# Hybrid encoder trunk: one modulation sum of the first layer moved from two half tiles ahead of a PSUM pool's closing to behind the half tile that follows the closing

## The chip, the cores and the metric

The kernel runs on one core of one Trainium2 chip. The metric is the device time of one launch in microseconds (us), as the median of the runs shown. One further launch was taken with the hardware profiler; the rows quoted below come from it, and times in rows count from the start of its span.

## The reference

Two layers on 1024 tokens of width 1024, one batch. In each layer a condition vector gives six modulation vectors (shift, scale and gate, for attention and for the feed-forward part); the input is normalised and modulated; ONE projection makes queries, keys and values of three head groups (A neighbourhood, B sliding window, C dense); each group's attention, a norm, an output projection and a gated sum follow, and then a gated SwiGLU part.

```python
cond = jax.nn.silu(c)
for l in range(DEPTH):
    mod = cond @ w_mod[l] + b_mod[l]
    sh_a, sc_a, gt_a, sh_f, sc_f, gt_f = [m[:, None, :] for m in split_cols(mod, (D,) * 6)]
    h = rms_norm(x, g_attn[l]) * (1 + sc_a) + sh_a
    proj = h @ w_in[l]
...
    x = x + gt_a * (y @ w_o[l])
    h = rms_norm(x, g_ffn[l]) * (1 + sc_f) + sh_f
...
    x = x + gt_f * ((jax.nn.silu(gate) * up) @ w_down[l])
return rms_norm(x, g_final)
```

## The kernel before, in words

Every matrix product is made of three TensorE (PE) passes, since each operand is split in a high and a low part (`mm3`: high by high, low by high, high by low). A product's PSUM tile fills one of the eight banks.

**The stage around the change** is the last part of the projection in the first layer (`l == 0`), in which the columns of groups A and B are projected. Column tiles `oc` 2 to 7, each in two halves of 512 tokens, make twelve half tiles, numbered `i = 2 * (oc - NE) + half`, 0 to 11 (two of them were computed earlier, in the start of the kernel). For each half tile:

- `ab_proj` makes 24 matmuls 128x512 into a PSUM tile `ps_ab` (8 pieces of the sum, 3 passes each);
- `ab_split` has ScalarE (ACT) cast the high part out of that PSUM tile into `qko`, and VectorE (DVE) subtract to get the low part. That DVE instruction, `qko<-ps_ab,qko`, is the tile's last reader and sets its bank free;
- `store` puts `qko` into DRAM (`qkd`), with DMAs that ACT's queue issues one half tile later, behind DVE's instruction;
- at the first half of each column tile, `split_tile` prepares the next tile's weights: ACT casts `whi`, DVE subtracts `wlo`.

**The modulation** of later stages is computed between these on DVE, which has time left. `mod_one` loads one block of 128 rows of `w_mod` (`wmt`, 512 KB, three buffers) and adds it, times the condition, to `acc` (128x1024). After the eighth block it splits `acc` into `acch` and `accl`. `mod_sum` then adds up the 128 partitions: four PE matmuls by a matrix of ones into two PSUM tiles `ps_mod`, and on DVE, twice, a product by the identity into `own` and a reduction into `sums`, and at the end a small addition into `mods`. A table sets for each half tile how many `mod_one` follow, and a tuple sets at which half tiles a `mod_sum` stands.

**The order is written by hand.** In this stage the five engines are pinned: what stands first in the code stands first in the engine's queue, and each engine works through its queue in order. An instruction that waits holds up all that stands behind it on that engine.

**Two PSUM pools.** Half tiles up to 7 take their tiles from a pool `psl` of eight banks. At `oc == 6`, first half (`i == 8`), this pool is closed, and two others open in its banks: `psS` with two tiles of two banks for the scores `sC`, and a new `psl` with four banks. A tile of a new pool waits for the last reader of what stood in its bank.

```python
1201         def mod_sum():
...
1204             l_, g, hi, lo = sums_due.pop(0)
...
1207             for o in (0, H):
1208                 ps = psl.tile([P, 4, P], F32, name="ps_mod", tag="mm")
...
1325                 if oc == 6 and half == 0:
1326                     close(ps_cm)
1327                     psS_cm, psS = open_pool("psS", bufs=2, space=PSUM)
1328                     ps_cm, psl = open_pool("ps2", bufs=4, space=PSUM)
...
1331                 ps = None if early else ab_proj(w, half)
...
1339                 if i in ((2, 6, 10) if l else (3, 6, 10)):
1340                     mod_sum()
```

With `oc == 7` (`i` 10 and 11) the first scores of group C stand in front of the half tile (`early_scores`): eight matmuls into two `sC` tiles, two maxima on DVE (`vecs<-sC`), two exponentials on ACT (`pr`, then `wst`), a reciprocal on DVE, and a division on GpSimd (POOL). After half tile 11 the four-bank pool closes too, and `opened` begins with attention of group C: transposes `T` (three banks), scores, and products `pv` (one bank).

Of the kernel before, what the change touches and what calls it, by code (L numbers as in the profile page):

```python
# [85 lines left out]
def trunk(ctx: ExitStack, tc, A, C, out):  # L86
# [9 lines left out]
    def open_pool(name, bufs=1, side="left", space=None):  # L96
        kw = dict(name=name, bufs=bufs, side=side, reuse_waits="tile")
        if space is not None:
            kw["space"] = space
            if space == PSUM:  # L100
                kw.pop("side")
        cm = tc.tile_pool(**kw)
        p = cm.__enter__()
        return cm, p

    def close(cm):
        cm.__exit__(None, None, None)
# [45 lines left out]
    def split_tile(st, a=1, hl=None, eng=None, scale=None):  # L153
        pl, tag, bufs = hl or (wp, "whl", 8)
        hi = pl.tile([P, 1024], F32R, name="whi", tag=tag, bufs=bufs)
        lo = pl.tile([P, 1024], F32R, name="wlo", tag=tag, bufs=bufs)
        if scale is None:
            act.copy(hi, st)
            (eng or pool).tensor_tensor(out=lo, in0=st, in1=f32(hi), op=ALU.subtract)
        else:  # L160
            act.activation(hi, st, AF.Copy, scale=scale)
            eng.scalar_tensor_tensor(
                out=lo, in0=st, scalar=scale, in1=f32(hi), op0=ALU.mult, op1=ALU.subtract
            )
        return parts(hi, a), parts(lo, a)
# [565 lines left out]
    def w_ab(l, oc):  # L731
        st = stage()
        c0 = oc * P if oc < 4 else 768 + (oc - 4) * P
        sp.dma_start(
            parts(st, KC), A["w_in"][l, :, c0 : c0 + P].rearrange("(k p) n -> p k n", p=P)
        )
        return st
# [167 lines left out]
    for l in range(2):  # L905
# [23 lines left out]
        def ab_proj(w, half):  # L929
            c = slice(half * H, (half + 1) * H)  # L930
            ps = psl.tile([P, 512], F32, name="ps_ab", tag="mm")
            for k in range(KC):
                mm3(ps, w[0][:, k], w[1][:, k], hh[:, k, c], hl[:, k, c], k == 0, k == 7)
            return ps

        def ab_split(oc, half, ps, pl):

            c = slice(half * H, (half + 1) * H)
            o = pl.tile([P, 2, H], F32R, name="qko", tag="qko", bufs=2)
            hi, lo = o[:, 0, :], o[:, 1, :]  # L940
            if oc < 4:
                hi, lo = (t.rearrange("p (j r i) -> p r j i", j=8, r=8) for t in (hi, lo))
                ps = ps.rearrange("p (r j i) -> p r j i", r=8, j=8)
                act.copy(hi, ps)
                sub(lo, ps, f32(hi))
            else:
                sc = -0.125 if oc < 7 else 1.0
                act.activation(hi, ps, AF.Copy, scale=sc)
                dve.scalar_tensor_tensor(
                    out=lo, in0=ps, scalar=sc, in1=f32(hi), op0=ALU.mult, op1=ALU.subtract  # L950
                )

            def store(eng=sp):
                for j in range(2):
                    to, v = qkd[oc, j], f32(o[j * 64 : j * 64 + 64])
                    if oc < 4:
                        to = to.rearrange("z p (j h n) -> h p z j n", h=2, n=64)[half]
                        v = v.rearrange("p z (j n) -> p z j n", n=64)
                        for z in range(2):
                            eng.dma_start(to[:, z], v[:, z])  # L960
                    else:
                        eng.dma_start(to[:, :, c].rearrange("z p t -> p z t"), v)

            return store
# [210 lines left out]
        def z_step():  # L1175
            if z_steps:
                what, h = z_steps.pop(0)
                what(h)
# [5 lines left out]
        def mod_one():  # L1184
            l_, g = todo[0]
            k = going["step"]
            if k == 0:
                going["acc"] = cp.tile([P, 1024], F32, name="acc", tag="acc")
            acc = going["acc"]
            mod_step(l_, g, k, acc, wm)  # L1190
            going["step"] = (k + 1) % KC
            if k == KC - 1:
                todo.pop(0)
                hi, lo = (
                    wp.tile([P, 1024], F32R, name=f"acc{p}", tag="whl", bufs=8) for p in "hl"
                )
                dve.tensor_copy(hi, acc)
                dve.tensor_tensor(out=lo, in0=acc, in1=f32(hi), op=ALU.subtract)
                sums_due.append((l_, g, hi, lo))

        def mod_sum():


            l_, g, hi, lo = sums_due.pop(0)
            sums = cp.tile([P, 8], F32, name="sums", tag="sums")
            own = wp.tile([P, 1024], F32, name="own", tag="whl", bufs=8)
            for o in (0, H):
                ps = psl.tile([P, 4, P], F32, name="ps_mod", tag="mm")
                row = ps.rearrange("p a b -> p (a b)")
                pe.matmul(row, onesr, hi[:, o : o + H], start=True, stop=False)  # L1210
                pe.matmul(row, onesr, lo[:, o : o + H], start=False, stop=True)
                d = own[:, o : o + H].rearrange("p (a b) -> p a b", a=4)
                dve.tensor_tensor(out=d, in0=ps, in1=bc(ident[:, None, :], [P, 4, P]), op=ALU.mult)
                n = o // P
                dve.tensor_reduce(out=sums[:, n : n + 4], in_=d, axis=AX.X, op=ALU.add)
            mod_finish(l_, g, sums)
# [86 lines left out]
        def early_scores():  # L1303

            p = len(first_pairs)
            if p == 0:
                prs = [
                    wp.tile([P, 1024], F32, name="pr", tag="whl", bufs=8),
                    cp.tile([P, 1024], F32, name="pr", tag="acc"),
                ]  # L1310
            else:
                prs = [stage(), stage()]
            rs = vecs[0][:, 8 * p : 8 * p + 8]
            for c in range(2):
                c_scores(0, 2 * p + c, c, prs[c], rs)
            first_pairs.append(prs)
            return lambda: divide(prs, rs)

        for oc in range(NE, 8):
            w = wab  # L1320
            for half in range(2):
                if half == 0 and oc < 7:
                    sc = -0.125 if oc < 3 else None
                    wab = split_tile(wst.pop(0), KC, eng=dve, scale=sc)
                if oc == 6 and half == 0:
                    close(ps_cm)
                    psS_cm, psS = open_pool("psS", bufs=2, space=PSUM)
                    ps_cm, psl = open_pool("ps2", bufs=4, space=PSUM)
                scored = early_scores() if oc == 7 else None
                early = l == 0 and half == 0 and oc in EARLY_AB  # L1330
                ps = None if early else ab_proj(w, half)
                if store:
                    store(sp if oc == 7 and half else act)
                if scored:
                    scored()
                if half == 0 and oc < 6:
                    wst.append(w_ab(l, oc + 2))
                i = 2 * (oc - NE) + half
                if i in ((2, 6, 10) if l else (3, 6, 10)):
                    mod_sum()  # L1340
                z_step()
                for _ in range(
                    (1, 1, 1, 1, 1, 1, 1, 1, 2, 2, 0, 0)[i]
                    if l else (0, 1, 0, 1, 2, 2, 2, 2, 2, 0, 0, 0)[i]
                ):
                    mod_one()
                store = None if early else ab_split(oc, half, ps, ab)
# [419 lines left out]
        for n in range(-AHEAD - 1, N + 3):  # L1767
# [84 lines left out]
            for end, (chunks, width) in norms.items():  # L1852
                if begins[end] <= m <= end and (m - begins[end]) % 8 == 7 and (n <= NC or m >= NC):
                    i = (m - begins[end]) // 8
# [569 lines left out]
        for u in range(NU):  # L2424
            i, t = divmod(u, NB)
# [164 lines left out]
```

## Time and profile before

| | |
|---|---|
| median of 3 runs | 2373.5 us |
| lowest and highest of them | 2372.1 and 2374.26 us |
| the profiled execution, whole | 2373.83 us |
| its span, first to last instruction | 2372.1 us |
| PE busy, its share of the span | 2327.3 us, 98% |
| DVE busy | 1755.5 us, 74% |
| ACT busy | 1184.2 us, 50% |
| POOL busy | 775.7 us, 33% |
| mean granted TensorE clock | 0.997 |

A timeline row gives start, duration, engine, operation, output<-inputs with shapes, the number of instructions merged, and in brackets how long the engine had stood idle before it and what ended that. PE rows of a single 128x512 matmul have a duration of 0.39 us but start 0.23 us apart, since matmuls overlap; the distance of starts is what counts. In rows all code has line L49, a helper that issues every instruction; groups are told apart by tile names. 1.73 us of the profiled execution (2373.83 less 2372.1) lie outside its span.

### The profile page before, as it was taken

Reading aid. Unit: us, or ns where it says so; the run is one execution under the profiler, and the core shown is the slowest. Engines: PE = TensorE matmul, PEld = TensorE weight load, DVE = VectorE, ACT = ScalarE, POOL = GpSimd, SP = SyncE. Lnnn points to the kernel's source line nnn. Section 1 sums busy time; section 2 is a strip of 40 time slices with the busy share of each in tenths; the row PEclk is TensorE's granted clock in tenths of the full one; section 3 lists DMA queues with packets and bytes.
Section 4 is the critical chain, followed back from the end, with each engine's and each line's share of the span. In section 5 each row is a group of like instructions: output and inputs, shape, how many; then the busy total and the mean of one; then the engine's idle time right before and its main releaser. Section 6 shows DMA issues by size and latency. Waiting matters only on the chain. (4 is left out here: it accounts for less than half of the span.)

```text
span 2372.1 us, 33468 instructions
## 1 busy us (share of the span) xinstructions
PE 2327.3 (98%) x11804; PEld 1960.9 (83%) x11804; DVE 1755.5 (74%) x2753; ACT 1184.2 (50%) x2261; POOL 775.7 (33%) x747
## 2 busy tenths in 40 slices
PE   9999999999999999999999999999999999999998
PEld 7887888888788888788888889988878888888886
DVE  6877998868857687596767689897796674537765
ACT  4422888844543333344533158896454334334443
POOL 1530356710344444200145124574005444430001
PEclk9999999999999999999999999999999999999999
DMA  8666507163345444686434861332634443239743
GB/s 279 182 204 199 156 5 210 39 212 107 111 155 164 152 142 151 201 248 186 153 102 128 252 187 28 91 104 89 221 98 130 154 153 103 98 105 294 213 120 112
DMA packets 307417, 358.02 MB, mean 151 GB/s; under 512 B 51996, under 2 KB 223868, under 8 KB 307248
## 3 DMA queue, kind: packets, MB, share of 16 engines
q1 hardware_dynamic: 290752, 346.26, 47.0%
q10 hardware_dynamic: 16128, 9.44, 1.5%
q8 instruction: 93, 1.52, 0.3%
q14 instruction: 76, 0.62, 0.1%
q0 software_dynamic: 368, 0.17, 0.0%
HBM read 270.84 MB, written 88.63 MB: 152 GB/s over the span
## 5 line engine op out<-in xcount | busy, mean ns | idle before, releaser
L49 PE MATMUL ps_d<-wpt 128*128 128x512 f32 x1848 | 423.7, 390 | 1.0 <-ACT wpt L49 0.7
L49 PEld LDWEIGHTS ps_d<-wpt 128*128 128x128 f32 x1848 | 345.7, 188 | 74.3 <-issue 3.0
L49 POOL TENSOR_SCALAR pr<-pr,rs 128x1024 f32<-128x1024 f32 (+2 forms) x248 | 190.5, 783 | 186.6 <-DVE rs L49 169.3
L49 POOL TENSOR_TENSOR sg<-sg,u 128x512 f32<-128x512 f32 x82 | 118.3, 1444 | 348.4 <-ACT sg L49 221.6
L49 PE MATMUL pv<-pt,vs 128*128 128x256 f32 x1088 | 173.9, 296 | 14.1 <-DVE y L49 12.9
L49 DVE TENSOR_TENSOR pt<-T,pt 128x512 fp32r<-128x512 f32 x272 | 177.3, 679 | 7.0 <-ACT pt L49 5.9
L49 ACT CAST wpt<-w 128x512 fp32r<-128x512 f32 x154 | 95.6, 621 | 167.8 <-PE ps_d L49 151.6
L49 DVE SCALAR_TENSOR_TENSOR acc<-wmt,condT,acc 128x512 f32<-128x512 f32 (+1 forms) x98 | 116.1, 1191 | 78.5 <-DMA wmt<-in_w_mod_dram 77.6
L49 ACT CAST pt<-T 128x512 fp32r<-128x512 f32 x272 | 151.5, 585 | 42.5 <-PE T L49 41.1
L49 ACT COPY u<-ps_w 128x512 f32<-128x512 f32 x128 | 75.1, 587 | 191.7 <-PE ps_w L49 189.5
L49 POOL TENSOR_TENSOR wpt<-ws,wpt 128x512 fp32r<-128x512 f32 x80 | 110.9, 1387 | 179.8 <-ACT wpt L49 139.3
L49 DVE TENSOR_TENSOR wpt<-w,wpt 128x512 fp32r<-128x512 f32 x154 | 108.7, 706 | 79.8 <-ACT wpt L49 79.7
L49 PEld LDWEIGHTS pv<-pt,vs 128*128 128x128 f32 x1088 | 141.0, 189 | 26.7 <-DVE y L49 24.6
L49 PE MATMUL T<-identr,pr 128*128 128x128 f32 x1176 | 160.0, 273 | 0.9 <-ACT edge L49 0.5
L49 PEld LDWEIGHTS T<-identr,pr 128*128 128x128 f32 x1176 | 137.8, 140 | 15.7 <-ACT edge L49 1.1
L49 ACT CAST wpt<-ws 128x512 fp32r<-128x512 f32 x176 | 107.7, 622 | 52.0 <-issue 23.0
L49 ACT CAST wpt<-graw 128x512 fp32r<-128x512 f32 x154 | 95.0, 617 | 59.2 <-DMA graw<-gpd 51.8
L49 DVE TENSOR_TENSOR wpt<-graw,wpt 128x512 fp32r<-128x512 f32 x154 | 109.8, 713 | 18.1 <-ACT wpt L49 18.1
L49 DVE TENSOR_TENSOR wpt<-ws,wpt 128x512 fp32r<-128x512 f32 x96 | 84.4, 887 | 47.7 <-ACT wpt L49 47.4
L49 DVE TENSOR_TENSOR ws<-wr 128x512 f32<-128x512 f32 x88 | 80.9, 919 | 50.4 <-POOL wpt L49 46.6
L49 DVE TENSOR_REDUCE rs<-sC 128x1 f32<-128x1024 f32 x88 | 107.4, 1220 | 12.8 <-PE sC L49 11.5
L49 PE MATMUL ps_w<-h22h,wpt 128*128 128x512 f32 x352 | 108.9, 391 | 2.4 <-ACT u L49 1.4
(306 smaller groups left out, 5932.1 us busy)
## 6 DMA issues: line engine op xcount, KB each, us to landing
wr<-in_w_gu_dram SPq DMA_DIRECT2D x92, 512.0 KB, 4.3
gpd<-sg SPq DMA_DIRECT2D x154, 256.0 KB, 4.4
graw<-gpd SPq DMA_DIRECT2D x76, 512.0 KB, 3.9
w<-in_w_down_dram SPq DMA_DIRECT2D x110, 256.0 KB, 5.2
wmt<-in_w_mod_dram SPq DMA_DIRECT2D x48, 512.0 KB, 5.5
qk<-qkd SPq DMA_DIRECT2D x44, 512.0 KB, 7.2
wst<-in_w_o_dram SPq DMA_DIRECT2D x32, 512.0 KB, 4.2
wmt<-in_w_mod_dram SPq DMA_DIRECT2D x64, 256.0 KB, 4.0
```

Source lines behind the costliest of these rows:

```text
L49: ins = op(*args, **kwargs)
```

## The change

In the first layer the second of three modulation sums stands at half tile 8 instead of 6. The table of `mod_one` is as it was, and so are the second layer and the queues of ACT, POOL and SP (their instructions keep their order).

```diff
                 i = 2 * (oc - NE) + half
-                if i in ((2, 6, 10) if l else (3, 6, 10)):
+                if i in ((2, 6, 10) if l else (3, 8, 10)):
                     mod_sum()
```

On PE, from half tile 6 (`ps_ab_1816`) on; the rows are the first of each tile, with the engines that they wait for (24 matmuls of each `ps_ab` are cut to one or two). First before:

```order
L49 MATMUL ps_ab_1816<-hh_111,whi_1727 128x512 [waits PE_49,Activation_49]
...
L49 MATMUL ps_mod_1847<-acch_1768,onesr_73 128x512 [waits DVE_49,PE_49]
L49 MATMUL ps_mod_1847<-accl_1769,onesr_73 128x512 [waits DVE_49]
L49 MATMUL ps_mod_1852<-acch_1768,onesr_73 128x512 [waits PE_49]
L49 MATMUL ps_mod_1852<-accl_1769,onesr_73 128x512
L49 MATMUL ps_ab_1867<-hh_111,whi_1727 128x512 [waits PE_49]
...
L49 MATMUL ps_ab_1914<-hh_111,whi_1812 128x512 [waits DVE_49]
```

Then with the change:

```order
L49 MATMUL ps_ab_1816<-hh_111,whi_1727 128x512 [waits PE_49,Activation_49]
...
L49 MATMUL ps_ab_1854<-hh_111,whi_1727 128x512 [waits PE_49]
...
L49 MATMUL ps_ab_1901<-hh_111,whi_1812 128x512 [waits PE_49,Activation_49]
L49 MATMUL ps_ab_1901<-hh_111,wlo_1813 128x512 [waits DVE_49]
...
L49 MATMUL ps_mod_1930<-acch_1768,onesr_73 128x512
L49 MATMUL ps_mod_1930<-accl_1769,onesr_73 128x512
L49 MATMUL ps_mod_1935<-acch_1768,onesr_73 128x512
L49 MATMUL ps_mod_1935<-accl_1769,onesr_73 128x512
```

The four matmuls of the sum moved past half tiles 7 (`ps_ab_1867`, now `ps_ab_1854`) and 8 (`ps_ab_1914`, now `ps_ab_1901`), and the waits in front of half tile 8 are others. In the built program before, half tile 7 lies in bank 4, and half tile 8, the first tile of the new four-bank pool, lies in bank 4 too: its wait on DVE is for `qko_1900<-ps_ab_1867`, the last reader of half tile 7. With the change half tile 7 lies in bank 1, and half tile 8 in bank 4, which held a `ps_mod` tile of the first sum; its waits are for PE's own matmuls of that sum, for ACT's `whi_1812` and for DVE's `wlo_1813`, the halves of its weights. The sum's two tiles lie in banks 7 and 6 of the new pool, and half tile 9 in bank 5.

On DVE, from the weights of half tile 8 (`wlo_1813`) on, first before (`qko_1864` and `qko_1900` read half tiles 6 and 7):

```order
L49 TENSOR_TENSOR wlo_1813<-wst_1760,whi_1812 128x1024
L49 TENSOR_TENSOR own_1846<-ps_mod_1847,identr_63 128x512
L49 TENSOR_REDUCE sums_1845<-own_1846 128x4
L49 TENSOR_TENSOR own_1846<-ps_mod_1852,identr_63 128x512
...
L49 SCALAR_TENSOR_TENSOR acc_1802<-wmt_1861,condT_79,acc_1802 128x1024
L49 SCALAR_TENSOR_TENSOR qko_1864<-ps_ab_1816,qko_1864 128x512
...
L49 SCALAR_TENSOR_TENSOR acc_1802<-wmt_1897,condT_79,acc_1802 128x1024
L49 SCALAR_TENSOR_TENSOR qko_1900<-ps_ab_1867,qko_1900 128x512
L49 TENSOR_TENSOR wlo_1904<-wst_1843,whi_1903 128x1024
L49 SCALAR_TENSOR_TENSOR acc_1802<-wmt_1941,condT_79,acc_1802 128x1024
```

Then with the change (`qko_1851` and `qko_1887` read half tiles 6 and 7, `qko_1951` half tile 8):

```order
L49 TENSOR_TENSOR wlo_1813<-wst_1760,whi_1812 128x1024
...
L49 SCALAR_TENSOR_TENSOR qko_1851<-ps_ab_1816,qko_1851 128x512
...
L49 SCALAR_TENSOR_TENSOR qko_1887<-ps_ab_1854,qko_1887 128x512
L49 TENSOR_TENSOR wlo_1891<-wst_1843,whi_1890 128x1024
L49 TENSOR_TENSOR own_1929<-ps_mod_1930,identr_63 128x512
L49 TENSOR_REDUCE sums_1928<-own_1929 128x4
...
L49 SCALAR_TENSOR_TENSOR acc_1802<-wmt_1941,condT_79,acc_1802 128x1024
L49 SCALAR_TENSOR_TENSOR acc_1802<-wmt_1944,condT_79,acc_1802 128x1024
L49 CAST acch_1947<-acc_1802 128x1024
L49 TENSOR_TENSOR accl_1948<-acc_1802,acch_1947 128x1024
L49 SCALAR_TENSOR_TENSOR qko_1951<-ps_ab_1901,qko_1951 128x512
```

The sum's five instructions moved past four `acc` steps, two `qko` and one `wlo`. In front of them now stands the wait for PE's sum behind half tile 8; behind them stand two `acc` steps, the two splits of `acc` and the last reader of half tile 8.

On PE again, where attention begins (`T` are the transposes of the first probabilities, `sC` scores); the last rows of the pieces show the waits, first before and then with the change:

```order
L49 MATMUL T_2133<-identr_63,pr_1984 128x128 [waits DVE_49,Pool_49]
L49 MATMUL T_2133<-identr_63,pr_1984 128x128 x3
L49 MATMUL T_2140<-identr_63,pr_1984 128x128 [waits DVE_49]
...
L49 MATMUL sC_2147<-qk_746 128x512 [waits Activation_49]
...
L49 MATMUL T_2152<-identr_63,pr_1985 128x128 [waits Pool_49]
...
L49 MATMUL T_2159<-identr_63,pr_1985 128x128 [waits DVE_49]
```

```order
L49 MATMUL T_2133<-identr_63,pr_1984 128x128 [waits DVE_49,Pool_49]
L49 MATMUL T_2133<-identr_63,pr_1984 128x128 x3
L49 MATMUL T_2140<-identr_63,pr_1984 128x128 x4
L49 MATMUL sC_2147<-qk_746 128x512 [waits Activation_49]
...
L49 MATMUL T_2152<-identr_63,pr_1985 128x128 [waits DVE_49,Pool_49]
...
L49 MATMUL T_2159<-identr_63,pr_1985 128x128 [waits DVE_49]
```

The order is the same, but `T_2152` waits for DVE as well. It lies in bank 5, which before held a tile of the third sum and with the change holds half tile 11; the wait is for that half tile's last reader. `T_2140` (bank 6) had to wait for the last reader of half tile 10, which now lies in bank 7.

## The prediction

> **What bounds the kernel now.** I read the page first, then the waits of PE, then the timeline of PE, DVE and ACT around the closing of the eight-bank pool.
>
> ```profile
> span 2372.1 us, 33468 instructions
> PE 2327.3 (98%) x11804; PEld 1960.9 (83%) x11804; DVE 1755.5 (74%) x2753; ACT 1184.2 (50%) x2261; POOL 775.7 (33%) x747
> ```
>
> PE is busy for 98% of the span, so the kernel's time is PE's work and PE's waits. The second view says who makes PE wait (total, times, longest):
>
> ```profile
> PE pv L49 <- DVE y L49: 12.9, 22, 1.3
> ...
> PE ps_ab L49 <- DVE qko L49: 4.1, 1, 4.1
> ```
>
> The first is 22 short waits in attention. The second is one wait of 4.1 us, the longest that PE has, and it is of this stage. The timeline of PE shows its place:
>
> ```profile
> 195.71 0.39 PE L49 MATMUL ps_mod<-acch,onesr 128*128 128x512 f32 x1
> ...
> 196.64 0.39 PE L49 MATMUL ps_ab<-hh,whi 128*128 128x512 f32 x1
> ...
> 201.85 0.39 PE L49 MATMUL ps_ab<-hl,whi 128*128 128x512 f32 x1
> 206.36 0.79 PE L49 MATMUL ps_ab<-hh,whi 128*128 128x512 f32 x1 [4.11 <-DVE qko L49]
> ...
> 209.49 0.39 PE L49 MATMUL ps_ab<-hh,wlo 128*128 128x512 f32 x1
> ...
> 218.81 1.98 PE L49 MATMUL sC<-qk 128*128 128x512 f32 x8
> 220.62 0.39 PE L49 MATMUL ps_ab<-hh,whi 128*128 128x512 f32 x1
> ```
>
> The sum that is moved starts at 195.71, half tile 7 at 196.64, and half tile 8, the first of the four-bank pool, at 206.36. Eight matmuls take 1.81 us (218.81 to 220.62), 0.2265 each, so half tile 7 was through at 201.85 + 0.23 = 202.08, and PE lost 206.36 - 202.08 = **4.28 us**. Behind the gap it is slow as well; a table of two stretches shows busy times and, behind POOL's, the granted clock:
>
> ```profile
> 202.30:206.30 4.00, 0.00 (x0) 0.00 (x0) 3.20 (x5) 1.53 (x2) 0.00 (x0) 0.97 0.90 264
> 206.30:209.50 3.20, 3.14 (x8) 2.48 (x9) 2.22 (x2) 0.00 (x0) 0.00 (x0) 0.51 1.00 374
> ```
>
> The clock is 0.51 from 206.3 to 209.5. The 48 matmuls of half tiles 8 and 9 take 218.81 - 206.36 = 12.45 us where 48 x 0.2265 = 10.87 are needed: **1.58 us** more. Gap and slow stretch cost 5.86 us together.
>
> Why the gap is there, DVE and ACT tell:
>
> ```profile
> 188.57 0.69 DVE L49 CAST acch<-acc 128x1024 fp32r<-128x1024 f32 x1
> ...
> 190.44 0.68 DVE L49 SCALAR_TENSOR_TENSOR qko<-ps_ab,qko 128x512 fp32r<-128x512 f32 x1
> ...
> 194.10 1.23 DVE L49 TENSOR_TENSOR wlo<-wst,whi 128x1024 fp32r<-128x1024 f32 x1 [0.24 <-ACT whi L49]
> 196.37 0.69 DVE L49 TENSOR_TENSOR own<-ps_mod,identr 128x512 f32<-128x512 f32 x1 [1.04 <-PE ps_mod L49]
> ...
> 199.22 2.60 DVE L49 SCALAR_TENSOR_TENSOR acc<-wmt,condT,acc 128x1024 f32<-128x1024 f32 x2
> 201.74 0.68 DVE L49 SCALAR_TENSOR_TENSOR qko<-ps_ab,qko 128x512 fp32r<-128x512 f32 x1
> 202.34 1.27 DVE L49 SCALAR_TENSOR_TENSOR acc<-wmt,condT,acc 128x1024 f32<-128x1024 f32 x1
> ...
> 205.62 0.68 DVE L49 SCALAR_TENSOR_TENSOR qko<-ps_ab,qko 128x512 fp32r<-128x512 f32 x1
> ```
>
> ```profile
> 202.45 1.25 ACTq L49 DMA_DIRECT2D qkd<-qko  x2
> 203.83 0.60 ACT L49 ACTIVATE qko<-ps_ab 128x512 fp32r<-128x512 f32 x1 [5.52 <-DVE acc L49]
> ```
>
> The sum holds DVE from 196.37 to 199.22 (2.85 us), two `acc` steps follow, and only at 201.74 is half tile 6 read. ACT stores it (202.45) and then casts half tile 7 (203.83), and DVE reads that at 205.62 to 206.30. PE starts at 206.36: bank 4 was half tile 7's.
>
> **The change, part by part.** *The wait at half tile 8 goes.* By the order, half tile 8 now waits for PE's own earlier sum and for its weights, `wlo_1813`, which stand on DVE ahead of all that moves, and were made from 194.10 to 195.33. So half tiles 7 and 8 follow each other without a gap: 7 from 195.71, 8 from 195.71 + 5.44 = 201.15, the sum at 206.59 for 0.93 us (195.71 to 196.64), half tile 9 from 207.52 to 212.96. Its bank (5) and the sum's (7, 6) were free long ago. The scores then end at 214.77 instead of 220.62: **5.86 us** ahead, and slow matmuls with the gap gone too. The next scores need half tile 7's reader; with four `acc` (1.3 each, 199.22 x2) and two `qko` from 195.3 on, even the stores and loads between leave it ready by 206, and PE comes at 212.96.
>
> *The sum's work is not saved.* Its four matmuls cost PE 0.93 us in both places. On DVE its 2.85 us now stand at the head of a chain: DVE waits until 206.59 + 0.66 (195.71 to 196.37) = 207.25 for PE's sum. I cost this wait itself at nothing: what stands ahead of it (two half tiles' readers, four `acc`, a `wlo`) fills DVE to about 205, and PE has 24 matmuls beside it. Loads for the two `acc` behind it are issued as earlier `acc` free buffers, and land in
>
> ```profile
> DMA to landing us min/median/max: 3.8/6.1/6.5
> ```
>
> at most 6.5 us; the later of the two loads needs the buffer of the `acc` of 202.34, which ended at 203.6, so even at the old times both are there by 210.1, as DVE reaches them.
>
> *Behind the sum the readers come late.* 207.25 + 2.85 (sum) + 2.60 (two `acc`) + 1.87 (splits, 188.57 to 190.44) puts half tile 8's reader at 214.57. ACT stores it and casts half tile 9 2.09 us later (201.74 to 203.83). Rows of what follows before:
>
> ```profile
> 219.64 0.69 DVE L49 SCALAR_TENSOR_TENSOR qko<-ps_ab,qko 128x512 fp32r<-128x512 f32 x1 [4.75 <-ACT qko L49]
> ...
> 223.86 0.17 DVE L49 RECIPROCAL vecs<-vecs 128x2 f32<-128x2 f32 x1 [1.27 <-ACT pr L49]
> 226.73 0.69 DVE L49 TENSOR_TENSOR own<-ps_mod,identr 128x512 f32<-128x512 f32 x1 [2.70 <-PE ps_mod L49]
> ...
> 230.16 0.69 DVE L49 SCALAR_TENSOR_TENSOR qko<-ps_ab,qko 128x512 fp32r<-128x512 f32 x1 [0.29 <-issue]
> ...
> 235.09 0.69 DVE L49 SCALAR_TENSOR_TENSOR qko<-ps_ab,qko 128x512 fp32r<-128x512 f32 x1 [0.54 <-ACT qko L49]
> 235.70 1.28 DVE L49 TENSOR_TENSOR pt<-T,pt 128x512 fp32r<-128x512 f32 x2
> ```
>
> ```profile
> 219.01 0.60 ACT L49 ACTIVATE qko<-ps_ab 128x512 fp32r<-128x512 f32 x1 [4.84 <-PE ps_ab L49]
> ```
>
> DVE follows ACT's cast by 0.63 (219.01 to 219.64): half tile 9 is read at 214.57 + 2.72 = 217.29, ahead of before by only 2.35 where PE is ahead by 5.86. Maxima, exponentials and the reciprocal keep this distance: reciprocal at 221.51. PE's third sum is ready at 226.73 - 5.86 = 220.87, so the third sum now starts behind the reciprocal, at 221.68, and the 2.7 us of slack that DVE had there are what makes good most of the delay. From its start to the next `qko` it was 3.43 (226.73 to 230.16); in the second layer, where it follows the reciprocal closely, with POOL dividing beside it, it was 3.07:
>
> ```profile
> 1384.45 0.69 DVE L49 TENSOR_TENSOR own<-ps_mod,identr 128x512 f32<-128x512 f32 x1 [1.60 <-PE ps_mod L49]
> ...
> 1387.52 0.69 DVE L49 SCALAR_TENSOR_TENSOR qko<-ps_ab,qko 128x512 fp32r<-128x512 f32 x1
> ```
>
> So half tile 10 is read at 224.75 to 225.11, which is 5.41 to 5.05 ahead of before, and DVE and ACT keep that into attention.
>
> *There PE is held.*
>
> ```profile
> 234.26 1.04 PE L49 MATMUL T<-identr,pr 128*128 128x128 f32 x8
> ...
> 236.05 1.04 PE L49 MATMUL T<-identr,pr 128*128 128x128 f32 x8
> ```
>
> PE reaches the second eight transposes (`T_2152`, `T_2159`) at 236.05 - 5.86 = 230.19. `T_2152` now waits for half tile 11's reader, at 235.78 less 5.41 to 5.05 = 230.37 to 230.73. `T_2159`, 0.4 behind, waits for the first `pt` as before, whose end was 236.34 and is 230.93 to 231.29, against 230.59 of PE. PE loses 0.34 to 0.70; below that nothing if DVE's chain is a little quicker, above it 1 us for each us that the chain is late. I take 0.7, by the first layer's own row. From there on PE is 5.86 - 0.7 = **5.2 us** ahead, all other engines 5.05 to 5.4, and nothing of the rest is tied to an absolute time.
>
> The sum, made against the profiled execution: 2373.83 - 5.2 = 2368.6. That lies 0.33 above the median shown, so against the median: 2373.5 - 5.2 = **2368.3 us**.
>
> **The rivals.** *The chain hides (2367.6).* PE's 5.86 come out whole, if DVE's chain is 0.7 quicker than I add up. For it: each step was taken from rows with small idle times in them. Against: already before, `T_2159` met the end of the first `pt` with 0.1 us to spare, so any lag of DVE shows.
>
> *The slow stretch isn't a constant (2369.9).* The clock fell just ahead of PE's restart and rose 3.1 us later; elsewhere gaps of one length had two outcomes:
>
> ```profile
> 32.05 2.07 PE L49 MATMUL ps_c<-whi,hh 128*128 128x512 f32 x4 [1.33 <-ACT hh L49]
> ```
>
> ```profile
> 435.93 0.74 PE L49 MATMUL pv<-pt,vs 128*128 128x256 f32 x4 [1.33 <-DVE y L49]
> ```
>
> Behind 1.33 us of idle time four matmuls took 2.07 us the one time (about twice 4 x 0.2265 and an end) and were at full pace the other. If the fall hangs on when the gap comes and not only on its length, typical executions pay less than 1.58 for this gap; without it the change brings 4.28 - 0.7 = 3.6 us, 2373.5 - 3.6 = 2369.9. For it: the three runs spread over 2.2 us. Against: the lowest of them alone is as far below the profiled execution as that stretch is long. [...]
>
> *PE meets the late readers more often (2370.5).* Between 214.8 and 228.4 PE also waits for half tile 8's bank (its second `ps_mod` tile), for the exponentials (second scores) and for half tile 9's bank. By the chain these come with 5.4, 0.6 and 5.0 us to spare; an ACT queue with 1 to 3 us more in it (stores that now fall between exponentials) uses up the smallest and leaves 2.2 to 4.2 us of the gain.
>
> *The sum at the head of DVE's queue costs more than the gap (2379, slower).* DVE stands idle before it until PE is through 28 matmuls, and behind it are two loads, two readers and ACT's exponentials. PE feels each us of it from 0.35 us of lateness on, at `T_2152`. The 5.2 are gone when the chain is 5.2 later than I have it, and 2379 needs 10 us, for which both `wmt` loads would have to land 10 us behind the time that the landing row allows. I see no such row.
>
> **How the numbers follow.** About 0.2% (4.7 us) is what a measurement of this kernel can tell from no change. My forecast, 2367.8 to 2368.9, gets 0.48; the hidden chain 0.10; the slow stretch 0.24; late readers, or a gap that stays for a reason I do not see, 0.13; slower than before by any mechanism 0.05. Faster by over 0.2% means below 2368.75: most of the forecast (0.45) and the hidden chain, 0.55. Within 0.2%: 0.03 + 0.24 + 0.13 = 0.40. Slower by over 0.2%: 0.05. The range goes from the hidden chain less the scatter of the median (2366.8) to the middle of the late readers (2371.0).
>
> **What would show it.** In the changed kernel's profile half tile 8 should follow half tile 7 with no idle time near 201.1, at clock 1.00; `own` should start near 207.2 with a wait for `ps_mod`; half tile 8's reader near 214.6 and the reciprocal near 221.5; the first transposes at 228.4; a new wait of 0.2 to 0.7 us of `T` on `qko` or `pt` near 230; and the span should be near 2366.9. I am wrong if PE waits at half tile 8 for anything, if a wait of over 1 us stands between 206 and 234, or if the 5.2 us are there at 240 and lost by the end.

## The result, and the profile after

The changed kernel took **2370.09 us** (median of 14 runs, 2368.25 to 2374.81) against 2374.6 us for the kernel before (14 runs, 2372.1 to 2378.17): ratio 0.9983, 95% interval 0.9975 to 0.999. That is 4.5 us less; the forecast was 5.2. The profiled execution took 2368.57 us as a whole, 5.3 us less than the profiled execution before.

The page's first lines, and the waits of PE (total, times, longest):

```profile
span 2366.8 us, 33472 instructions
PE 2325.0 (98%) x11804; PEld 1959.9 (83%) x11804; DVE 1756.6 (74%) x2753; ACT 1184.7 (50%) x2261; POOL 775.7 (33%) x747
```

```profile
PE pv L49 <- DVE y L49: 13.3, 23, 1.3
PE ps_w L49 <- ACT sg L49: 3.4, 5, 1.3
```

Before, the second of these read:

```profile
PE ps_w L49 <- ACT sg L49: 2.1, 5, 0.7
```

The wait of 4.1 us of `ps_ab` for `qko` is gone from the list and none is listed from 190 to 240. The waits of `ps_w` for `sg`, fifth in the list before, are now second: they have grown from 2.1 to 3.4 us, to which we return. The timeline of PE at the same place:

```profile
200.57 0.39 PE L49 MATMUL ps_ab<-hl,whi 128*128 128x512 f32 x1
200.80 0.39 PE L49 MATMUL ps_ab<-hh,whi 128*128 128x512 f32 x1
...
206.25 0.39 PE L49 MATMUL ps_mod<-acch,onesr 128*128 128x512 f32 x1
...
207.17 0.39 PE L49 MATMUL ps_ab<-hh,whi 128*128 128x512 f32 x1
...
212.62 1.98 PE L49 MATMUL sC<-qk 128*128 128x512 f32 x8
...
214.43 0.39 PE L49 MATMUL ps_ab<-hh,whi 128*128 128x512 f32 x1
```

Half tile 8 starts at 200.80, one matmul's distance (0.23) behind the last of half tile 7. The sum stands at 206.25, half tile 9 at 207.17, and the scores end at 214.43 where they ended at 220.62. The table of the two stretches, with the clock behind POOL's busy time:

```profile
202.30:206.30 4.00, 4.00 (x20) 3.29 (x19) 3.02 (x3) 0.23 (x1) 0.00 (x0) 1.00 0.68 234
206.30:209.50 3.20, 3.20 (x16) 2.63 (x15) 2.53 (x4) 0.60 (x1) 0.00 (x0) 1.00 0.47 125
```

The clock is 1.00 in both, where it was 0.97 and 0.51. On DVE:

```profile
203.75 0.68 DVE L49 SCALAR_TENSOR_TENSOR qko<-ps_ab,qko 128x512 fp32r<-128x512 f32 x1
...
206.91 0.69 DVE L49 TENSOR_TENSOR own<-ps_mod,identr 128x512 f32<-128x512 f32 x1 [1.34 <-PE ps_mod L49]
...
214.26 0.68 DVE L49 SCALAR_TENSOR_TENSOR qko<-ps_ab,qko 128x512 fp32r<-128x512 f32 x1
216.97 0.69 DVE L49 SCALAR_TENSOR_TENSOR qko<-ps_ab,qko 128x512 fp32r<-128x512 f32 x1 [2.03 <-ACT qko L49]
...
221.20 0.17 DVE L49 RECIPROCAL vecs<-vecs 128x2 f32<-128x2 f32 x1 [1.27 <-ACT pr L49]
221.28 0.67 DVE L49 TENSOR_TENSOR own<-ps_mod,identr 128x512 f32<-128x512 f32 x1
...
224.34 0.69 DVE L49 SCALAR_TENSOR_TENSOR qko<-ps_ab,qko 128x512 fp32r<-128x512 f32 x1
...
229.05 0.69 DVE L49 SCALAR_TENSOR_TENSOR qko<-ps_ab,qko 128x512 fp32r<-128x512 f32 x1 [0.32 <-ACT qko L49]
```

Half tile 7's reader ends at 203.75 + 0.68 = 204.43, 1.9 us earlier than before but still 3.6 us behind half tile 8's start. PE no longer waits for it. The first transposes of attention:

```profile
228.07 1.04 PE L49 MATMUL T<-identr,pr 128*128 128x128 f32 x8
...
229.89 1.16 PE L49 MATMUL T<-identr,pr 128*128 128x128 f32 x8
```

The second group takes 1.16 where it took 1.04: the new wait at `T_2152` and `T_2159` is 0.12 us, not 0.7.

To see where the time came from and went, the start of each PE matmul of before was compared with that of the same matmul after, each from its trace's first matmul. PE leads by 0.34 us at 190, by 6.19 at 216, and by 5.29 at the end. So the place of the change brought **5.85 us**, and 0.90 were given back later. The 0.34 us that it leads by at 190 arose in the first 60 us, ahead of anything that was changed.

### The profile page after: what moved, and what is told of

It reads as the page before. It is cut to its first block, busy times and chain, and to the rows that moved or that the text cites. A ratio compares the mean times of both kernels' runs of the same rounds, so it can differ in the third digit from the quotient of the medians.

```text
span 2366.8 us, 33472 instructions
## 1 busy us (share of the span) xinstructions
PE 2325.0 (98%) x11804; PEld 1959.9 (83%) x11804; DVE 1756.6 (74%) x2753; ACT 1184.7 (50%) x2261; POOL 775.7 (33%) x747
## 5 line engine op out<-in xcount | busy, mean ns | idle before, releaser
L49 PE MATMUL ps_w<-ht3h,wpt 128*128 128x512 f32 x352 | 108.8, 390 | 2.4 <-ACT sg L49 2.4
```

What stands on the lines that cost most here:

```text
L49: ins = op(*args, **kwargs)
```

## Experiments

Three questions: is it the bank, or DVE's relief, that closes the gap? Does the slow stretch of the clock belong to the gap? And why do the medians show 4.5 us where the place shows 5.85? Each kernel's ratio is to runs of the kernel before taken beside it. Where said, all runs of a kernel are put together (104 of the kernel before, taken beside the changed kernel and the experiments; 25 of the changed one), and their means compared, with 95% intervals from resampling the runs. A trace is of one execution, and not always a typical one: that of e2 is the slowest of its eleven.

### The bank or VectorE

**e1, the sum left at 6, half tile 7 in another bank.**

```diff
+                if l == 0 and 2 * (oc - NE) + half == 7:
+                    for _ in range(1):
+                        skip = psl.tile([P, 512], F32, name="skip", tag="mm")
+                        pe.matmul(
+                            skip[:, 0:P], hh[:, 0, 0:P], hh[:, 0, 0:P],
+                            start=True, stop=True,
+                        )
                 ps = None if early else ab_proj(w, half)
```

> The second sum stays at half tile 6, as in the kernel before. One small extra matmul (128x128, result unused) takes bank 4 of the eight-bank pool just ahead of half tile 7, so half tile 7 goes to bank 5 and half tile 8 finds bank 4 free. Theory (the shared bank): the 4.28 us gap ahead of half tile 8 goes, though VectorE is as late as before (reader of half tile 7 still ends near 206.3), and with it the slow stretch behind it where there is one; 4.3 to 5.9 us below the kernel before, some 2369.5 to 2370.5 against its 2374.6. Rival (VectorE is relieved by moving the sum): the sum hasn't moved, so the gap stays; 2374.6, ratio 1.000.

Measured: 2371.11 us (11 runs), 0.9982 of the kernel before (0.9974 to 0.9991). PE, the table of stretches, and half tile 7's reader on DVE:

```profile
202.06 0.39 PE L49 MATMUL ps_ab<-hl,whi 128*128 128x512 f32 x1
202.28 0.39 PE L49 MATMUL ps_ab<-hh,whi 128*128 128x512 f32 x1
```

```profile
202.30:206.30 4.00, 4.00 (x19) 3.34 (x18) 3.05 (x4) 1.54 (x2) 0.00 (x0) 1.00 0.89 295
206.30:209.50 3.20, 3.20 (x15) 2.65 (x15) 2.55 (x3) 0.00 (x0) 0.00 (x0) 1.00 1.00 335
```

```profile
205.83 0.68 DVE L49 SCALAR_TENSOR_TENSOR qko<-ps_ab,qko 128x512 fp32r<-128x512 f32 x1
```

The sum did not move, and the reader ends at 206.51 (before: 206.30), yet the gap is gone. The rival falls: DVE's relief is not needed. The median is 0.6 us above the expected band; in the profiled execution that lead is lost later in the kernel (below).

**e2, the changed kernel with half tile 7 back in bank 4** (the edit is against the changed kernel).

```diff
+                if l == 0 and 2 * (oc - NE) + half == 7:
+                    for _ in range(2):
+                        skip = psl.tile([P, 512], F32, name="skip", tag="mm")
+                        pe.matmul(
+                            skip[:, 0:P], hh[:, 0, 0:P], hh[:, 0, 0:P],
+                            start=True, stop=True,
+                        )
```

> The changed kernel with its sum at half tile 8, and two small extra matmuls (128x128, results unused) that take banks 1 and 0 ahead of half tile 7, so that half tile 7 lands in bank 4 again, the bank of half tile 8. Theory (the shared bank): half tile 8 waits for the reader of half tile 7, which in the changed kernel ended at 204.43, while TensorE came to half tile 8 at 200.80: a gap of some 3.6 us comes back, and a slow stretch of up to 1.6 us with it; 3.6 to 5.2 us over the changed kernel, 2373.7 to 2375.3. Rival (VectorE is relieved by moving the sum): no gap over 0.5 us, 2370.1 as the changed kernel.

Measured: 2373.88 us (11 runs), 1.0 of the kernel before (0.9991 to 1.0009). PE, then DVE, then the clock behind the gap:

```profile
204.80 0.39 PE L49 MATMUL ps_ab<-hl,whi 128*128 128x512 f32 x1
210.05 0.80 PE L49 MATMUL ps_ab<-hh,whi 128*128 128x512 f32 x1 [4.86 <-DVE qko L49]
```

```profile
208.10 1.28 DVE L49 SCALAR_TENSOR_TENSOR acc<-wmt,condT,acc 128x1024 f32<-128x1024 f32 x1 [2.12 <-DMA wmt<-in_w_mod_dram]
209.31 0.68 DVE L49 SCALAR_TENSOR_TENSOR qko<-ps_ab,qko 128x512 fp32r<-128x512 f32 x1
```

```profile
210.00:213.20 3.20, 3.15 (x8) 2.51 (x8) 1.12 (x1) 0.00 (x0) 0.00 (x0) 0.50 0.71 190
```

With the bank shared the gap is back although the sum is out of the way: the reader now stands behind an `acc` that waited 2.12 us for its load. Moving the sum without freeing the bank buys nothing.

**e5, the sum at 7, still ahead of the closing** (`(3, 7, 10)` in the tuple).

> The second sum stands behind half tile 7, still ahead of the closing of the eight-bank pool. Half tile 7 then lies in bank 1, and bank 4, which half tile 8 takes, is that of the sum's second product. Theory (the shared bank): half tile 8 waits for VectorE's second product of the sum; by the changed kernel's rows TensorE ends the sum at 201.73 and VectorE that product at 203.6, so a gap of some 1.9 us stays: 1.9 us over the changed kernel if the clock holds, 3.5 us if a slow stretch follows a gap of this length too; 2372.0 to 2373.6. Rival (what helps is that the sum is out of VectorE's way ahead of half tile 7's reader): any place behind half tile 7 would do, and the time is the changed kernel's, 2370.1.

Measured: 2373.3 us (11 runs), 0.999 of the kernel before (0.9982 to 0.9999). PE, DVE, and the clock behind the gap:

```profile
201.62 0.39 PE L49 MATMUL ps_mod<-accl,onesr 128*128 128x512 f32 x1
203.74 0.47 PE L49 MATMUL ps_ab<-hh,whi 128*128 128x512 f32 x1 [1.73 <-DVE own L49]
```

```profile
202.92 0.68 DVE L49 TENSOR_TENSOR own<-ps_mod,identr 128x512 f32<-128x512 f32 x1
```

```profile
204.00:208.00 4.00, 4.00 (x19) 3.29 (x19) 3.93 (x6) 0.00 (x0) 0.00 (x0) 1.00 0.35 98
```

Half tile 8 now waits for the sum's second product: 203.74 - 201.85 = 1.89 us, as worked out ahead, and no slow stretch follows here. That gives 2372.0; the median is 1.3 us above it, and the profiled execution loses as much and more behind the place (the table below). The three together settle the first question: whoever last reads bank 4 ahead of the closing sets half tile 8's start.

### The slow stretch

**e7, the gap filled with work.**

```diff
                     ps_cm, psl = open_pool("ps2", bufs=4, space=PSUM)
+                    if l == 0:
+                        fill = psS.tile([P, 1024], F32, name="fill", tag="S")
+                        for _ in range(18):
+                            pe.matmul(
+                                fill[:, 0:512], hh[:, 0, 0:P], hh[:, 0, 0:H],
+                                start=True, stop=True,
+                            )
```

> The kernel before, with 18 extra matmuls (128x128 by 128x512, results unused) between half tiles 7 and 8, worth 18 x 0.227 = 4.1 us: the wait for bank 4 stays as long as it is, but TensorE is not idle in it. If the slow stretch follows the idle gap in every execution, this saves its 1.58 us in the median: 2373.0 against 2374.6, and the clock record shows 1.00 through 200 to 215. If the slow stretch was the profiled execution's alone, or comes in a part of the executions, the median moves by 0 to 0.8 us: 2373.8 to 2374.6.

Measured: 2373.05 us (11 runs), 0.9992 of the kernel before (0.9983 to 1.0001); against all runs of before the mean is 2.1 us lower (1.3 to 2.8), where 1.58 was expected. PE and the clock:

```profile
203.22 4.24 PE L49 MATMUL fill<-hh 128*128 128x512 f32 x18
207.59 0.50 PE L49 MATMUL ps_ab<-hh,whi 128*128 128x512 f32 x1
```

```profile
207.00:211.00 4.00, 3.87 (x18) 2.87 (x17) 2.95 (x3) 0.00 (x0) 0.00 (x0) 1.00 0.97 349
```

PE waits just as long for bank 4, but is not idle, and the clock holds. None of the 90 runs of before taken beside the experiments has a mean clock above 0.997; 6 of these 11 have 0.998.

**c1, the kernel before, profiled again** (no edit).

> The kernel before, profiled once more. If the slow stretch behind the gap follows the gap, the clock record shows a stretch at 0.50 that begins within 4 us of the gap's end at 206.3 again, beside whatever stretches the start has; if it was the first profile's own, the clock is 1.00 from 200 to 215 with the gap there.

Measured: one run, 2375.55 us.

```profile
207.81 0.50 PE L49 MATMUL ps_ab<-hh,whi 128*128 128x512 f32 x1 [4.05 <-DVE qko L49]
```

```profile
207.80:211.00 3.20, 3.19 (x10) 2.54 (x11) 2.28 (x2) 0.00 (x0) 0.00 (x0) 0.68 0.99 361
```

Gap and slow stretch are there again; the stretch begins about 1 us behind the gap's end and not ahead of it, and lasts as long (3.4 us in the clock record of both traces). A third profile with this gap (f1, below) has it too. The stretch belongs to the gap; what the traces show of where it begins stands in the last section.

### What is given back later

**e9, the changed kernel again** (no further edit), and **e6 and e10, the sum at 9**, each a kernel with `(3, 9, 10)`.

> The changed kernel once more, 4.5 to 4.9 us below the kernel before. If the 1.1 us that its first profile lost near 760 us (ActivationE's sg came late) follow from the change, they are there again; if they were that execution's own, the place shows 0.2 to 0.6 us of waiting as in the kernel before, and other waits have moved.

> The second sum stands one half tile later still, behind half tile 9. Theory (the shared bank): the sum need only stand behind the closing of the eight-bank pool, so half tile 8 starts without a gap as in the changed kernel; 2370.1 plus or minus 0.5. Rival (late readers): each half tile by which the sum is later makes VectorE's chain behind it later, and the first transposes of attention are held by 0.5 to 1 us more: 2370.6 to 2371.1.

> The kernel with the sum behind half tile 9 once more, beside the changed kernel on the same chip. If its median of 2368.4 against 2370.1 was the scatter of few executions, the two now lie within 1 us of each other, either sign; if the later place is better by a mechanism, it is lower by 1 to 2 us again, and its profile shows where TensorE gains over the changed kernel behind half tile 9.

Measured: e9 2371.95 us (11 runs), 0.9987 of before (0.9979 to 0.9996): 3.2 us below the kernel before beside it, where 4.5 to 4.9 were expected. e6 2368.43 (9 runs), 0.9975 (0.9966 to 0.9985); e10 2368.96 (10 runs), 0.9976 (0.9966 to 0.9985). Put together, the sum at 9 is 1.9 us below the changed kernel (0.8 to 2.9; 19 runs and 25), the best version here, and lower than either expectation for e6. "Late readers" falls: half tile 8 starts without a gap, and the later sum holds nothing up.

**e8, PE made late by what the change saved** (the edit is against the changed kernel).

```diff
+                if l == 0 and 2 * (oc - NE) + half == 7:
+                    fill = psl.tile([P, 512], F32, name="fill", tag="mm")
+                    for _ in range(26):
+                        pe.matmul(
+                            fill, hh[:, 0, 0:P], hh[:, 0, 0:H],
+                            start=True, stop=True,
+                        )
```

> The changed kernel with 26 extra matmuls (128x128 by 128x512, result unused) ahead of half tile 7, 26 x 0.227 = 5.9 us of TensorE work with no gap: it makes TensorE late by what the change saved, without the wait and without the slow stretch. If every stage behind follows TensorE one for one, 5.9 us over the changed kernel, 2376.0. If later waits (on transfers and on ActivationE) give back part of what a lead or a delay of TensorE brings, as the medians' 4.5 to 4.9 us against 5.86 at the place itself suggest, some 4.7 us over it, 2374.8.

Measured: 2375.21 us (11 runs), 0.9998 of before (0.9989 to 1.0007). Against all runs of the changed kernel its mean is 3.9 us higher (2.5 to 5.2): PE's 5.9 us of extra work cost less than 5.9, and nearer to the second expectation (4.7) than to the first.

Where a lead is lost, the traces show. In all of them the starts of the same matmuls were compared with the first profile of before (us; added matmuls are left out, and with the sum at 9 its 0.91 us of PE, which stand behind 216, are taken off the gain). The last three columns are of one load in the second layer's attention, whose rows follow, counted from its issue: the start of a packet of 16 KB, the landing of the load's last part, and PE's wait.

| kernel | lead gained, 190 to 216 | change of lead, 216 to 2350 | of it 1500 to 1560 | 16 KB packet | last part | PE's wait |
|---|---|---|---|---|---|---|
| before | - | - | - | 3.56 | 9.71 | 0.72 |
| before, c1 | -0.13 | -0.06 | -0.06 | 3.62 | 9.84 | 0.84 |
| changed | 5.85 | -0.90 | -0.10 | 3.71 | 9.91 | 0.90 |
| changed, e9 | 5.85 | -2.81 | -1.54 | 2.09 | 11.32 | 2.34 |
| e1 | 5.71 | -4.61 | -4.25 | 2.00 | 12.44 | 3.44 |
| sum at 9, e6 | 5.88 | -0.66 | -0.01 | 3.41 | 9.61 | 0.61 |
| sum at 9, e10 | 5.88 | -0.46 | -0.04 | 3.89 | 9.79 | 0.79 |
| sum at 7, e5 | 3.87 | -3.57 | -2.93 | 2.09 | 11.10 | 2.11 |
| e2 | -1.46 | 0.20 | -0.03 | 1.23 | 9.29 | none |
| e7 | 1.34 | -0.21 | -0.01 | -3.38 | 8.35 | none |
| e8 | -0.05 | -0.22 | -0.02 | -4.93 | 8.65 | none |

The six profiles that gained 3.9 us or more at the place all give something back, 0.5 to 4.6 us; the four that gained less hold what they have within 0.22. In e9, e1 and e5 the largest part lies at one row, first of before, then of e9 and of e1:

```profile
1535.06 0.83 PE L49 MATMUL sA<-qk 128*128 128x256 f32 x4 [0.72 <-DMA qk<-qkd]
```

```profile
1532.11 0.82 PE L49 MATMUL sA<-qk 128*128 128x256 f32 x4 [2.34 <-DMA qk<-qkd]
```

```profile
1533.31 0.89 PE L49 MATMUL sA<-qk 128*128 128x256 f32 x4 [3.44 <-DMA qk<-qkd]
```

PE waits for the keys and queries of the next head. A wait of up to 0.9 costs next to nothing (0.00 to 0.10 in the table): the scores behind it start 11.98 us after the load's issue in before, with a wait of 0.72, and 11.99 in e7, with none. A longer wait costs about 0.8 us less than its length (2.34 in e9 cost 1.54). In e1 and e5 it costs 1.6 us more than that, and the clock record shows a slow stretch behind it as well (mean clock 0.96 from 1500 to 1545 in both, 1.00 in e9).

**f1, f2, f3: before, changed and sum at 9, with a load left out.** They leave out the keys of head 1, which are set to zero, so that head's part of the output is missing. The same edit in each:

```diff
         def load_k(t, oc, j):
             src = qkd[oc, j].rearrange("z p t -> p z t")
+            if l == 1 and oc == 2 and j == 1:
+                pool.memset(f32(t[:, 0:2, :]), 0.0)
+                return [t[:, 0, :], t[:, 1, :]]
```

> The kernel before, with one load left out far behind the change: in the second layer's attention the keys of head 1 of the first group (2 x 512 KB) are set to zero by GpSimd instead of being loaded, so TensorE no longer waits at 1535 us for that load. Left out: that head's real keys, and so its part of the output. That wait was 0.7 us in the profile of the kernel before and 0.8 to 3.4 us in those of the kernels without the gap. Theory (the load gives back part of the lead): the kernel before gains little, 0.3 to 1 us. Rival (the wait is scatter of the load, whatever runs ahead of it): it gains as much as the changed kernel does.

> The changed kernel with the same load left out. Theory (the load gives back part of the lead): it gains 1.5 to 2 us over the changed kernel, and stands 5.5 to 5.9 us below the kernel before with that load left out, the whole of what the place itself showed. Rival (scatter): the difference to the kernel before with that load left out stays at the medians' 4.2 to 4.8 us.

> The sum behind half tile 9, with the same load left out. If the 1.9 us by which it was faster than the changed kernel came from that wait (0.8 us there against 0.9 and 2.3 in the two profiles of the changed kernel), it is now within 0.7 us of the changed kernel with the load left out; if they came from elsewhere, it is 1.5 to 2 us lower again.

Measured (11 runs each): f1 2375.63, f2 2370.51, f3 2370.59; of before 1.0005 (0.9996 to 1.0014), 0.9981 (0.9972 to 0.9989) and 0.9978 (0.9969 to 0.9987). The wait is gone in all three, as in f2:

```profile
1530.24 0.84 PE L49 MATMUL sA<-qk 128*128 128x256 f32 x4
```

But the edit leaves out another load than the one that PE waited for. In the profile of before the keys of head 1 were issued at 1511.25, had landed by 1518.54, and were first read at 1525.03, with no wait. The load that ends PE's wait at 1535.06 is that of the next head, issued at 1525.22, and f1 to f3 still make it. So they show what the kernels take where this wait is absent, and not that a missing load is what removed it.

From 1500 to 1560 their lead changes by -0.03 to -0.05, and from 216 to 2350 it grows, by 1.65, 0.47 and 1.35. The changed kernel's mean is here 5.6 us below that of before (4.3 to 6.9), the size that the place itself showed; with the wait, over all runs, 4.1 (3.2 to 4.9). Sum at 9 and changed kernel are then alike (0.1 us, -1.4 to 1.2). Both would fit the theory that the wait takes back the lead in some executions, but they don't prove it. The two differences overlap. Half of the step between them comes from f1, which was to gain 0.3 to 1 us and stands 0.7 above the kernel before (-0.5 to 1.8); f2 gained 0.8 us over the changed kernel (-0.1 to 1.8) where 1.5 to 2 was expected; and f3 stands above e6 and e10 where it should not.

What goes with the wait can be read from the DMA records. The landing of the next head's queries, the last piece of that load, is reported in 16 parts. In e7 all land from 8.09 to 8.35 us after the load's issue; in e1 fourteen land by 8.78, and the last at 12.44. In the nine traces with a last part later than 9.2 us, those in the table but e7 and e8, a packet of 16 KB of the queue q8 (its kind is "instruction" in the profile) started 1.2 to 3.9 us after the issue. In the other five (e7, e8, f1 to f3) the packet started ahead of the issue, by 0.04 to 4.93 us, and the last part came at 8.35 to 8.65. So the load is late where this packet falls into it. That the packet is the cause is argued from this, not shown by an experiment. Nor does the lead alone set it: the load is issued as much earlier as PE is ahead (in e9 at 1520.65 against 1525.22, 4.6 us), the packet came at 3.56 and 3.62 in the two profiles of before, and at 3.71 and 2.09 in the two of the changed kernel.

Left open: what sets the packet's time, and whether the sum at 9 is better by a mechanism; its gain at the place is that of the changed kernel (5.88 and 5.85).

## Why the prediction was right, and where it was not

- **The gap: right.** 4.28 us of waiting went; half tile 8 was to start at 201.15, and did at 200.80 plus a lead of 0.34. The cause, bank 4, is shown by e1, e2 and e5. From 190 to 240 the list of PE's waits is now empty, which answers the rivals of late readers and of a costly sum.
- **The slow stretch: right for this gap.** 1.58 us went with the gap (4.28 + 1.58 = 5.86; the traces gave 5.85). The rival that made it an accident gave 2369.9, near the 2370.09 measured, but c1 and f1 have the stretch with this gap as well, and e7 loses it with the gap filled: a time that fits does not make a rival right. What that rival supposed was seen all the same: the stretch does not begin at one place against the gap (0.31 us ahead of its end in before, about 1 us behind it in c1), and the longer of two waits need not be the one with a stretch behind it (2.11 us in e5 had one, 2.34 us in e9 had none). The gaps of 4.05 us and more at this place had one in each of four profiles (the last section).
- **DVE's chain: right up to the reciprocal.** With the lead of 0.34 added, half tile 8's reader came at 214.60 (forecast 214.57), half tile 9's at 217.31 (217.29), the reciprocal at 221.54 (221.51).
- **The 0.7 us at the transposes: mis-sized.** It measured 0.12, so that the rival of the hidden chain was nearly right here. Two steps failed. From the third sum to the next `qko` I took 3.43, the first layer's row, between bounds of 3.43 and 3.07; it took 224.34 - 221.28 = 3.06. And half tile 11's reader of before (235.09) had itself waited for ACT, and ACT for PE: its exponentials ended at 234.16 + 0.19 = 234.35, PE's last matmul of the half tile at 234.03 + 0.40 = 234.43, and ACT's cast began at 234.46. Taking the chain's lead off it put the reader at 229.68 at the earliest, where it came at 229.05 + 0.34 = 229.39.
- **"Nothing of the rest is tied to an absolute time": this step failed.** It let the lead run through to the end. The runs don't show anything tied to an absolute time, but later waits took part of the lead, and the forecast put them at nothing. One of its own signs of being wrong came in part: net of the 0.34, PE led by 5.71 us at 240, by 4.95 at the end of the result's profile, and in e9 (net of 0.10) by 5.70 and 3.04. In the profile of the result 1.08 us went at 760, in the feed-forward part, where the same PE row waits for ACT, first before, then after:

```profile
765.70 0.73 PE L49 MATMUL ps_w<-ht3h,wpt 128*128 128x512 f32 x2 [0.23 <-ACT sg L49]
```

```profile
760.71 0.73 PE L49 MATMUL ps_w<-ht3h,wpt 128*128 128x512 f32 x2 [1.28 <-ACT sg L49]
```

In e9 that place lost 0.27 us, so most of the 1.08 was that execution's own, and the load at 1532 took 1.54. The two errors have opposite signs: 0.58 us too much were taken off at the transposes, and what later waits took was not taken off at all. That the span came out at 2366.8 where 2366.9 was forecast is luck to this extent. The medians show 4.5 us and not 5.2; that the later waits are the whole of the difference is not shown. The rest of the 1.8 us by which the median lies above the forecast is the base: the forecast stood on three runs of before (2373.5), of which 14 gave 2374.6. The time lies within the range, though above the 2367.8 to 2368.9 of the forecast itself.

## What to carry to other kernels

When a pool closes and another opens in its banks, look up who last reads the bank that the first new tile gets: a tile more or less ahead of the closing changes that, and one more small tile (e1) closed a gap that looked like a late engine. The gap on PE cost here its length (4.28 us) and about half of the slow stretch behind it (1.58 of 3.41 us), so it was worth more than the waits show. A lead won early need not be a lead at the end: look at the waits for loads and other engines that are nearly hidden, since some executions lost part of the lead there. And before leaving out a load to test a wait, check by issue and landing that it is the load that ends the wait.

## What the runs showed of the hardware

Gaps of 4.05 to 4.86 us at half tile 8 were followed by a slow stretch in four profiles of four (before, c1, f1, e2; in e2 one of 6.8 us), and so was the wait of 3.44 us in e1. Around 2 us both happened: the wait of 2.11 us in e5 had one behind it (mean clock 0.96 from 1500 to 1545), those of 2.34 us in e9 (1.00 there) and 1.73 us in e5 (1.00 from 204 to 208) had none.

The slow stretch of before runs from 206.05 to 209.46, 3.41 us at a clock of 0.50. PE's idle time in the 3.41 us ahead of each stretch's start (us; idle is where no matmul of the trace runs):

| trace, end of the wait | the wait | idle time in the 3.41 us ahead of the stretch | clock in the stretch |
|---|---|---|---|
| before, 206.36 | 4.11 | 3.41 | 0.5 |
| e1, 1533.31 | 3.44 | 2.80 | 0.5 |
| e2, 210.05 | 4.86 | 2.16 | 0.5 |
| f1, 210.18 | 4.14 | 2.43 | 0.5 |
| c1, 207.81 | 4.05 | 2.26 | 0.5 |
| e5, 1533.40 | 2.11 | 2.11 | 0.5 |

In e2 another 2.70 us of idle time lie in the first 3.41 us of the stretch. The length of the wait alone does not sort these cases, since the 2.34 us of e9 had no stretch behind them. What sets where a stretch begins, and why that wait had none, is left open.

Such stretches also stand in the first 50 us of every profile, 3.4 to 13.7 us of them in all, and differ between profiles of the same code: largely by them the leads over the first profile of before already run from -3.97 to 0.34 us at 190, ahead of anything that was changed.
